# A fourth of the down products' weight remainders made by an adding transfer

## The chip, the cores and the metric

The kernel runs on one core of a Trainium2 chip. The metric is the device time of one execution in microseconds.

## The reference, cut to what matters

One decoder layer on 256 tokens of width 2048, in float32: a SwiGLU feed-forward network (FFN), a mixer with gated linear attention and dilated attention, and a second FFN.

```python
def swiglu(x, w_gate, w_up, w_down):
    return (jax.nn.silu(x @ w_gate) * (x @ w_up)) @ w_down
...
x = x + 0.5 * swiglu(rms_norm(x, ffn1_norm), ffn1_w_gate, ffn1_w_up, ffn1_w_down)
h = rms_norm(x, mix_norm)
z = h @ w_in
...
x = x + concat(o_g, o_a) @ w_out
x = x + 0.5 * swiglu(rms_norm(x, ffn2_norm), ffn2_w_gate, ffn2_w_up, ffn2_w_down)
```

The down products are `(...) @ w_down`, with w_down of 5632 x 2048, once in each FFN.

## The kernel before, in words

All large products are made in float32 precision out of three products in a rounded format (fp32r). Each operand W is split into a rounded part Wh and a remainder Wl = W - Wh, and the same is done with the activations; TensorE then adds activation-high x Wh (L179), activation-high x Wl (L181) and activation-low x Wh (L183) into one bank of PSUM. The helper `split` (L87 to L90) makes the two parts: the scalar engine copies W into a rounded tile (L89), and the vector engine subtracts that from W (L90).

The weights come as 1 MB pairs of tiles. `prepare` (L127) starts the load of a pair `raw` on SyncE's queue when it reaches the first tile of the pair (k = 0, L149; three buffers of raw), and then splits one of its two tiles, 128 x 1024, into `wh` and `wl`, four buffers of each. `weights` (L159) keeps two more tiles ready ahead of the one that it hands out. A list `jobs` (L114) gives the order of all weights: first FFN gate and up, first FFN down, the mixer, second FFN gate and up, second FFN down.

`column_pair` (L191) goes over the inner dimension, one weight tile at a time. With a tile it makes twelve matmuls: two halves of the tokens (t), three products, two banks (j). For a gate/up pair the inner dimension is 16 tiles, and eleven such pairs follow each other. For the down products it is 44 tiles, and two passes make the 2048 columns, so 88 weight tiles in each FFN.

At the end of a gate/up pair, for each t, `evac` (L231) makes sg (scalar engine, L233), u and its block transpose us (vector engine, L234, L238), and GpSimd issues 16 small transfers `ur<-us` of 16 KB that finish the transpose (L241). `finish`, run later, splits ur into the activations uh and ul of the down products. The last of these 32 transfers of a pair therefore fall into the beginning of the next pair, and those of the eleventh pair into the beginning of the down products. The transfers of GpSimd's queue use eight completion semaphores in turn, and an issue waits until the transfer eight places before it has landed.

The instructions of each engine are put in order when the program is built, by a scheduler that goes by dependencies and its own costs; after that each engine takes its own in order.

Of the kernel before, what the change touches and what calls it, by code (L numbers as in the profile page):

```python
# [14 lines left out]
F32 = mybir.dt.float32  # L15
F32R = mybir.dt.float32r
U32 = mybir.dt.uint32
AF = mybir.ActivationFunctionType
ALU = mybir.AluOpType
# [17 lines left out]
def layer_kernel(tc, x, xT, gains, gla_gate_up, gla_gate_bias, gla_out_norm, att_q_norm, att_k_norm,  # L37
                 w_ff1, w_dn1, w_mix, w_low, w_out, w_ff2, w_dn2, c_sq, c_rope, c_mask, out):

    nc = tc.nc  # L40
# [3 lines left out]
    with ExitStack() as es:  # L44
# [42 lines left out]
        def split(dst_h, dst_l, src):  # L87

            nc.scalar.activation(dst_h, src, AF.Copy)  # L89
            nc.vector.tensor_sub(dst_l, src, dst_h.bitcast(F32))  # L90
# [30 lines left out]
        raws = [None]  # L121
        started = []

        def wtile(name):
            return wp.tile([P, 2, 512], F32R, name=name, tag=name, bufs=WBUF)

        def prepare():  # L127
            if not jobs:
                return
            job = jobs.pop(0)  # L130
            if job == "low":
                raw = wp.tile([P, KT, P], F32, name="raw", tag="raw", bufs=3)
                nc.sync.dma_start(raw, w_low.rearrange("p (k f) -> p k f", f=P))
                got = []
                for i in range(2):
                    w = wtile("wh").rearrange("p j f -> p (j f)").rearrange("p (k f) -> p k f", f=P)
                    nc.gpsimd.memset(w.bitcast(F32), 0.0)
                    split(w[:, :, 0:RANK], w[:, :, 64:64 + RANK], raw[:, 8 * i:8 * i + 8, 0:RANK])
                    got.append(w)
                ready.extend(got)  # L140
                return
            w, i, k = job
            if k == 0:
                raw = raws[0] = wp.tile([P, 2, 2, 512], F32, name="raw", tag="raw", bufs=3)
                flat = raw.rearrange("p k j f -> p (k j f)")
                parts = 1 if started else 4
                started.append(True)
                for c in range(0, 2048, 2048 // parts):
                    nc.sync.dma_start(flat[:, c:c + 2048 // parts], w[i, :, c:c + 2048 // parts])  # L149
            wh, wl = wtile("wh"), wtile("wl")  # L150
            if len(started) < 3:
                started.append(True)
                for j in range(2):
                    split(wh[:, j], wl[:, j], raws[0][:, k, j])
            else:
                split(wh, wl, raws[0][:, k])
            ready.append((wh, wl))

        def weights(early=False):  # L159
            if early:  # L160
                return prepare()
            while jobs and len(ready) <= AHEAD:
                prepare()
            return ready.pop(0)
# [511 lines left out]
```

## Time and profile before

| | before |
|---|---|
| median of 3 runs | 1766.66 us (1765.84 to 1767.97) |
| the profiled execution | 1767.72 us |
| its span in the profile | 1765.9 us |
| TensorE busy | 1757.9 us |
| VectorE busy | 994.3 us |
| ScalarE busy | 838.5 us |
| GpSimd busy | 375.3 us |
| granted TensorE clock, mean | 0.999 |

PE is TensorE, DVE the vector engine, ACT the scalar engine, POOL GpSimd, and SPq SyncE's queue of transfers. A row of a group ends with its busy time, the mean length of one instruction in ns, and the idle time of its engine just ahead of it with what ended that. The busy time of GpSimd counts the issue of a transfer, not its movement; the time from issue to landing stands in a list of its own.

### The profile page before, as it was taken

Reading aid. Unit: us, or ns where it says so; the run is one execution under the profiler, and the core shown is the slowest. Engines: PE = TensorE matmul, PEld = TensorE weight load, DVE = VectorE, ACT = ScalarE, POOL = GpSimd, SP = SyncE. Lnnn points to the kernel's source line nnn. Section 1 sums busy time; section 2 is a strip of 40 time slices with the busy share of each in tenths; the row PEclk is TensorE's granted clock in tenths of the full one; section 3 lists DMA queues with packets and bytes.
Section 4 is the critical chain, followed back from the end, with each engine's and each line's share of the span. In section 5 each row is a group of like instructions: output and inputs, shape, how many; then the busy total and the mean of one; then the engine's idle time right before and its main releaser. Section 6 shows DMA issues by size and latency. Waiting matters only on the chain.

```text
span 1765.9 us, 21578 instructions
## 1 busy us (share of the span) xinstructions
PE 1757.9 (100%) x8276; PEld 1535.6 (87%) x8276; DVE 994.3 (56%) x1045; ACT 838.5 (47%) x1014; POOL 375.3 (21%) x742
## 2 busy tenths in 40 slices
PE   9999999999999999999999999999999999999999
PEld 7888888888888888888888888888888888888887
DVE  6555555555544645566655666555555555544544
ACT  6444444444444544565754454444444444444442
POOL 0333343443400001011000000333333343410000
PEclk9999999999999999999999999999999999999999
DMA  8666666666655556555444455666666566565653
GB/s 335 211 218 213 216 214 219 207 225 220 213 213 197 193 210 209 193 198 212 167 167 163 148 193 197 218 214 216 215 214 218 212 220 213 212 215 211 219 211 119
DMA packets 74695, 365.45 MB, mean 207 GB/s; under 512 B 17200, under 2 KB 30512, under 8 KB 32352
## 3 DMA queue, kind: packets, MB, share of 16 engines
q1 hardware_dynamic: 50864, 350.25, 55.5%
q0 software_dynamic: 23008, 12.76, 2.5%
q8 instruction: 64, 1.05, 0.2%
q10 hardware_dynamic: 720, 1.07, 0.2%
q14 instruction: 39, 0.32, 0.0%
HBM read 350.38 MB, written 2.10 MB: 200 GB/s over the span
## 4 chain that ended last, share of the span: by engine, by line
PE 99%; DMA 1%; DVE 0%; ACT 0%; SPq 0%; issue 0%
PE acc L181 32%; PE acc L183 32%; PE acc L179 32%; PE tp L85 1%; DMA raw<-in_w_ff_dram 0%; PE tp L540 0%; PE tp L402 0%; PE tp L555 0%; DMA gT<-in_gains_dram 0%; PE tp L558 0%; PE acc L455 0%; PE acc L456 0%; PE tp L428 0%; PE tp L427 0%; PE tp L477 0%; PE tp L520 0%
## 5 line engine op out<-in xcount | busy, mean ns | idle before, releaser
L90 DVE TENSOR_TENSOR wl<-raw,wh 128x1024 fp32r<-128x1024 f32 (+1 forms) x658 | 800.6, 1221 | 708.9 <-ACT wh L89 708.4
L89 ACT ACTIVATE wh<-raw 128x1024 fp32r<-128x1024 f32 (+1 forms) x660 | 690.8, 1051 | 862.9 <-PE acc L183 846.3
L181 PE MATMUL acc<-wl,hh 128*128 128x512 f32 x1792 | 549.2, 381 | 0.1
L183 PE MATMUL acc<-wh,hl 128*128 128x512 f32 x1792 | 544.6, 381 | 0.0
L179 PE MATMUL acc<-wh,hh 128*128 128x512 f32 x1792 | 536.1, 381 | 2.3 <-ACT wh L89 2.3
L241 POOL DMA_DIRECT2D ur<-us x704 | 344.3, 497 | 574.4 <-ACT sg L233 404.7
L179 PEld LDWEIGHTS acc<-wh,hh 128*128 128x128 f32 x1792 | 338.3, 189 | 51.0 <-ACT wh L89 3.1
L181 PEld LDWEIGHTS acc<-wl,hh 128*128 128x128 f32 x1792 | 338.7, 189 | 49.0 <-issue 1.0
L183 PEld LDWEIGHTS acc<-wh,hl 128*128 128x128 f32 x1792 | 338.9, 189 | 47.8 <-DVE hl L276 0.2
L181 PE MATMUL acc<-wl,uh 128*128 128x512 f32 x704 | 212.4, 379 | 0.0
L183 PE MATMUL acc<-wh,ul 128*128 128x512 f32 x704 | 211.9, 379 | 0.0
L179 PE MATMUL acc<-wh,uh 128*128 128x512 f32 x704 | 210.7, 379 | 0.0
L183 PEld LDWEIGHTS acc<-wh,ul 128*128 128x128 f32 x704 | 133.1, 189 | 18.9
L181 PEld LDWEIGHTS acc<-wl,uh 128*128 128x128 f32 x704 | 133.1, 189 | 18.8
L179 PEld LDWEIGHTS acc<-wh,uh 128*128 128x128 f32 x704 | 133.0, 189 | 18.6
L106 POOL TENSOR_TENSOR rs<-a,mhalf 128x4 f32<-128x4 f32 (+1 forms) x12 | 17.5, 1455 | 257.0 <-DVE a L352 257.0
L320 POOL DMA_DIRECT2D rope<-in_c_rope_dram x1 | 0.7, 747 | 209.1 <-PE acc L183 209.1
L234 DVE SCALAR_TENSOR_TENSOR u<-acc,rt,sg 128x512 f32<-128x512 f32 x44 | 32.7, 744 | 0.0
L238 DVE STREAM_TRANSPOSE us<-u 128x512 f32<-128x512 f32 x44 | 31.3, 711 | 1.5
L106 POOL TENSOR_TENSOR rt<-ssum,mhalf 128x1 f32<-128x1 f32 x6 | 3.9, 644 | 123.9 <-DVE ssum L110 123.8
L233 ACT ACTIVATE sg<-acc,rt 128x512 f32<-128x512 f32 x44 | 29.8, 678 | 0.6
L90 DVE TENSOR_TENSOR ul<-ur,uh 128x512 fp32r<-128x512 f32 x44 | 30.1, 683 | 0.0
(151 smaller groups left out, 598.0 us busy)
## 6 DMA issues: line engine op xcount, KB each, us to landing
raw<-in_w_ff_dram SPq DMA_DIRECT2D x175, 1024.0 KB, 5.0
raw<-in_w_dn_dram SPq DMA_DIRECT2D x88, 1024.0 KB, 4.8
raw<-in_w_mix_dram SPq DMA_DIRECT2D x48, 1024.0 KB, 4.8
raw<-in_w_out_dram SPq DMA_DIRECT2D x16, 1024.0 KB, 4.8
ur<-us POOLq DMA_DIRECT2D x704, 16.0 KB, 3.9
xs<-in_x_dram SPq DMA_DIRECT2D x2, 1024.0 KB, 9.5
xt<-in_xT_dram SPq DMA_DIRECT2D x7, 256.0 KB, 6.8
raw<-in_w_ff_dram SPq DMA_DIRECT2D x4, 256.0 KB, 4.3
```

Source lines behind the costliest of these rows:

```text
L85: nc.tensor.transpose(dst, src, ident[:n, :n])
L89: nc.scalar.activation(dst_h, src, AF.Copy)
L90: nc.vector.tensor_sub(dst_l, src, dst_h.bitcast(F32))
L106: nc.gpsimd.tensor_tensor(dst, src, mhalf[:, :src.shape[-1]], op=ALU.pow)
L179: nc.tensor.matmul(ps[j], lhsT=sh, rhs=alt(wh[:, j, :]), start=first and i == 0, stop=False)
L181: nc.tensor.matmul(ps[j], lhsT=sh, rhs=alt(wl[:, j, :]), start=False, stop=False)
L183: nc.tensor.matmul(ps[j], lhsT=sl, rhs=alt(wh[:, j, :]), start=False, stop=last and i == len(ws) - 1)
L233: nc.scalar.activation(halves(sg), ps[0], AF.Silu, scale=rt[:, t:t + 1])
L234: nc.vector.scalar_tensor_tensor(halves(u), ps[1], rt[:, t:t + 1], halves(sg), op0=ALU.mult, op1=ALU.mult)
L238: nc.vector.transpose(us.rearrange("p (q j c) -> p j q c", q=4, j=4), u)
L241: nc.gpsimd.dma_start(ur[32 * q:32 * q + 32, r * P:(r + 1) * P], us[32 * r:32 * r + 32, q * P:(q + 1) * P])
L320: ld(rv, c_rope.rearrange("(t p) f -> p t f", p=P))
```

## The change

In the down products of both FFNs, for every second pair of tiles (i odd) the second tile (k = 1) is split in another way. The scalar engine copies W rounded into wh as before, copies -W rounded into wl, and GpSimd issues a transfer from raw onto wl that adds: wl becomes -Wh + W. The vector engine has no part in it. That is every fourth tile (tiles 3, 7, 11 and so on), 22 of the 88 in each FFN. The lines behind the new branch move down by five: L179, L181, L183, L233 and L241 of before are L184, L186, L188, L238 and L246 of after.

```diff
                 for j in range(2):
                     split(wh[:, j], wl[:, j], raws[0][:, k, j])
+            elif k and i % 2 and (w is w_dn1 or w is w_dn2):
+
+                nc.scalar.activation(wh, raws[0][:, k], AF.Copy)
+                nc.scalar.activation(wl, raws[0][:, k], AF.Copy, scale=-1.0)
+                nc.gpsimd.dma_start(wl.bitcast(F32), raws[0][:, k], accum_op=ALU.add)
             else:
                 split(wh, wl, raws[0][:, k])
             ready.append((wh, wl))
```

GpSimd's instructions from the first FFN to the mixer, before: the 352 small transfers of eleven pairs, then loads for the mixer.

```order
L106 ISA
L106 TENSOR_TENSOR rt<-ssum,mhalf 128x1 x2
L241 DMA ur<-us 32x128 x352
L320 DMA rope<-in_c_rope_dram 128x2x128
L321 DMA gq<-in_att_q_norm_dram 128x128
```

And now (wl<-raw is the adding transfer):

```order
L106 TENSOR_TENSOR rt<-ssum,mhalf 128x1 x2
L246 DMA ur<-us 32x128 x320
L159 DMA wl<-raw 128x1024
L246 DMA ur<-us 32x128 x32
L159 DMA wl<-raw 128x1024 x21
L325 DMA rope<-in_c_rope_dram 128x2x128
```

The first adding transfer (tile 3) stands ahead of the 32 small transfers of the eleventh pair, and the second (tile 7) with all the others behind them. The second FFN has the same rows.

The scalar engine around the end of the eleventh pair of the first FFN, before (sg is that pair's evacuation, uh its activations):

```order
L233 ACTIVATE sg<-acc,rt 128x512
L89 ACTIVATE wh<-raw 128x1024
L233 ACTIVATE sg<-acc,rt 128x512
L89 ACTIVATE wh<-raw 128x1024 x7
L89 ACTIVATE uh<-ur 128x4x128
L89 ACTIVATE wh<-raw 128x1024 x6
L89 ACTIVATE uh<-ur 128x4x128
```

And now (L158 is the negated copy):

```order
L238 ACTIVATE sg<-acc,rt 128x512
L158 ACTIVATE wl<-raw 128x1024
L157 ACTIVATE wh<-raw 128x1024
L238 ACTIVATE sg<-acc,rt 128x512
L89 ACTIVATE wh<-raw 128x1024 x3
L158 ACTIVATE wl<-raw 128x1024
L157 ACTIVATE wh<-raw 128x1024
L89 ACTIVATE wh<-raw 128x1024 x3
L89 ACTIVATE uh<-ur 128x4x128 x2
```

The negated copy stands ahead of the plain one of the same tile, and both splits of the last activations have moved to one place.

TensorE at tile 7 of the first FFN's down products, before (acc_3772 and acc_3773 are the banks of the first half of the tokens, acc_3780 and acc_3781 those of the second; wh_3856 and wl_3857 are tile 7):

```order
L179 MATMUL acc_3772<-wh_3856,uh_122 128x512
L179 MATMUL acc_3773<-wh_3856,uh_122 128x512
L181 MATMUL acc_3772<-wl_3857,uh_122 128x512
L181 MATMUL acc_3773<-wl_3857,uh_122 128x512
L183 MATMUL acc_3772<-wh_3856,ul_123 128x512
```

And now (tile 7 is wh_3857 and wl_3858):

```order
L184 MATMUL acc_3772<-wh_3857,uh_122 128x512
L184 MATMUL acc_3773<-wh_3857,uh_122 128x512
L184 MATMUL acc_3780<-wh_3857,uh_122 128x512
L184 MATMUL acc_3781<-wh_3857,uh_122 128x512
L186 MATMUL acc_3772<-wl_3858,uh_122 128x512
```

The remainder's first product has moved from the third to the fifth matmul of this tile. In the second FFN the same holds for tile 7 and for two later tiles of the adding kind, and at the very last tile the order of the last four was written anew; in the other tiles of the adding kind the remainder stands where it stood.

## The prediction

> **What bounds the kernel now.** I read the page first: busy times, the chain that ended last and the groups of the two engines that split the weights.
>
> ```profile
> span 1765.9 us, 21578 instructions
> ...
> PE 1757.9 (100%) x8276; PEld 1535.6 (87%) x8276; DVE 994.3 (56%) x1045; ACT 838.5 (47%) x1014; POOL 375.3 (21%) x742
> ...
> PE 99%; DMA 1%; DVE 0%; ACT 0%; SPq 0%; issue 0%
> ...
> L90 DVE TENSOR_TENSOR wl<-raw,wh 128x1024 fp32r<-128x1024 f32 (+1 forms) x658 | 800.6, 1221 | 708.9 <-ACT wh L89 708.4
> L89 ACT ACTIVATE wh<-raw 128x1024 fp32r<-128x1024 f32 (+1 forms) x660 | 690.8, 1051 | 862.9 <-PE acc L183 846.3
> ```
>
> The list of transfers (KB each, us from issue to landing at the end):
>
> ```profile
> raw<-in_w_dn_dram SPq DMA_DIRECT2D x88, 1024.0 KB, 4.8
> ...
> ur<-us POOLq DMA_DIRECT2D x704, 16.0 KB, 3.9
> xs<-in_x_dram SPq DMA_DIRECT2D x2, 1024.0 KB, 9.5
> ...
> rope<-in_c_rope_dram POOLq DMA_DIRECT2D x1, 128.0 KB, 2.5
> ```
>
> TensorE is busy for 1757.9 of 1765.9 us, so at most 8.0 us could be won by removing all its idle time. The vector engine sits idle waiting for the scalar engine, and the scalar engine waits for TensorE to give a weight buffer back (846.3 us). Both are ahead of TensorE, not behind it. Freeing the vector engine gives the kernel nothing; the question is only whether the new source of a remainder is as early as the old one.
>
> How early it must be is read from the timeline of TensorE at the start of the down products of the first FFN (columns: start, length, engine, line, operation, tiles, count).
>
> ```profile
> 465.73 0.59 PE L181 MATMUL acc<-wl,hh 128*128 128x512 f32 x2
> 466.16 0.59 PE L183 MATMUL acc<-wh,hl 128*128 128x512 f32 x2
> 466.59 0.59 PE L179 MATMUL acc<-wh,uh 128*128 128x512 f32 x2
> ...
> 474.79 0.59 PE L181 MATMUL acc<-wl,uh 128*128 128x512 f32 x2
> ...
> 484.72 0.59 PE L179 MATMUL acc<-wh,uh 128*128 128x512 f32 x2
> 485.15 0.59 PE L181 MATMUL acc<-wl,uh 128*128 128x512 f32 x2
> 485.58 0.59 PE L183 MATMUL acc<-wh,ul 128*128 128x512 f32 x2
> ```
>
> The down products start at 466.59. A weight tile is twelve matmuls; from tile 0 at 466.59 to tile 7 at 484.72 are 18.13 us, 2.59 us a tile. Four buffers are in turn: tile 3's remainder goes where the last gate/up tile's was, which is read until 465.73 + 0.59 = 466.32, and it is first read at 474.79. That is a budget of 8.47 us, the same for every fourth tile after.
>
> **The change, part by part.**
>
> *Removed:* 44 subtractions (22 in each FFN) of 1.22 us, 54 us of the vector engine, all beside TensorE: worth 0. *Added on the scalar engine:* 44 copies of -W, rounded, 1.05 us each, 46 us in two phases of 88 x 2.59 = 228 us on an engine that is busy for 47% of the span: 0 by themselves, but each lies in the budget above. *Added on the GpSimd queue:* 44 transfers of 512 KB, which must read W and -Wh and write the sum. No row shows one, so its time L from issue to landing is an unknown. The ends are the 128 KB rope load at 2.5 us and the 1 MB load of x in the crowded start, 9.5. The nearest row is a weight load, 4.8 us: it moves 1 MB once, and the new transfer reads twice 512 KB. I add 0.7 for GpSimd's longer issue (rows below) and for other loads in flight, and take **L = 5.5**.
>
> Beside that row stands a rule of the Trainium skill ("DMA: Bandwidth & Descriptors", Anatomy of one DMA): a transfer from GpSimd costs about 2.0 us fixed plus bytes at 436 GB/s. By it 512 KB would take an estimated 3.2 us and, with both sources counted, 4.4. It gives 4.4 for a weight load too, and the row has 4.8, so the row is taken; with 3.2 for L the forecast below would be some 4.6 us lower.
>
> *Does L fit in steady running?* The scalar engine, the vector engine and GpSimd at the same place show what a handover takes.
>
> ```profile
> 464.20 1.06 ACT L89 ACTIVATE wh<-raw 128x1024 fp32r<-128x1024 f32 x1 [1.53 <-PE acc L183]
> ...
> 465.29 1.23 DVE L90 TENSOR_TENSOR wl<-raw,wh 128x1024 fp32r<-128x1024 f32 x1 [1.36 <-ACT wh L89]
> ...
> 467.21 0.71 DVE L238 STREAM_TRANSPOSE us<-u 128x512 f32<-128x512 f32 x1
> ...
> 468.46 4.88 POOL L241 DMA_DIRECT2D ur<-us  x10 [20.35 <-ACT sg L233]
> 474.69 4.89 POOL L241 DMA_DIRECT2D ur<-us  x10 [1.34 <-DMA ur<-us]
> 481.24 5.98 POOL L241 DMA_DIRECT2D ur<-us  x12 [1.66 <-DMA ur<-us]
> ```
>
> And GpSimd's groups of issues (busy time, mean ns of one):
>
> ```profile
> L241 POOL DMA_DIRECT2D ur<-us x704 | 344.3, 497 | 574.4 <-ACT sg L233 404.7 <-DMA ur<-us 80.2 <-issue 76.7
> ...
> L320 POOL DMA_DIRECT2D rope<-in_c_rope_dram x1 | 0.7, 747 | 209.1 <-PE acc L183 209.1
> ```
>
> In the timeline the transpose ends at 467.92 and the first issue begins at 468.46: 0.54 us. So 8.47 - 1.05 (the copy) - 0.54 - 0.15 (two handovers; from the scalar to the vector engine, 465.26 to 465.29, it took 0.03, and I estimate twice that or more from a transfer's landing) leaves **6.7 us for L**. At 5.5 it fits: 0. It also holds raw longer than the subtraction did. Raw has three buffers, so the copy of the next tile in that buffer is five tiles (12.95 us) behind; the release after 1.05 + 0.54 + 5.5 = 7.1 and a load of 4.8 make 11.9, so 0 is taken there too.
>
> *The queue it is put on.* GpSimd issues in order. Behind the last gate/up column pair stand the 32 small transfers of its two halves (the timeline's rows above: 10 + 10 + 12), and in the changed program the first accumulating transfer (tile 3) is ahead of all 32, the second (tile 7) behind all 32. Before, only the splits of the last activations waited for them, which the down products read at the end of a pass (tiles 40 to 43). They end at 481.24 + 5.98 = 487.22. Tile 7's remainder is wanted earlier: in the new order it is that tile's fifth matmul, at 485.58. So it is late before it is even issued, by 487.22 - 485.58 = 1.64 us.
>
> How the first transfer moves the 32: its negated copy can start at 466.32, ends about 467.4, and is issued about 467.95, for about 0.6 us, so the small ones start near 468.5, as now. They use eight completion semaphores in turn, so the eighth behind it waits for it to land, at 467.95 + 5.5 = 473.45, where now it starts near 468.46 + 7 x 0.497 = 471.94: 1.5 later. Part of that falls into the waits of 1.34 and 1.66 us that are there already. The ends are 3.0 earlier (both waits gone) and 4 later (a landing of 8 us); I take **1.0 later**.
>
> Tile 7 then: 1.64 + 1.0 + 5.5 + 0.1 (to TensorE) = **8.2 us** in which TensorE stands. Queued behind that waiting matmul is everything TensorE has; nothing else can fill in, since it takes its matmuls in order.
>
> The same place in the second FFN:
>
> ```profile
> 1533.72 0.59 PE L179 MATMUL acc<-wh,uh 128*128 128x512 f32 x2
> ...
> 1552.71 0.59 PE L183 MATMUL acc<-wh,ul 128*128 128x512 f32 x2
> ...
> 1552.07 2.44 POOL L241 DMA_DIRECT2D ur<-us  x5 [0.21 <-issue]
> ```
>
> The small transfers end at 1554.51, the fifth matmul of tile 7 is at 1552.71: 1.80 + 6.6 = **8.4 us**.
>
> *What a stop of TensorE costs beyond itself.* The only stop of the run in full work is at its start, 1.99 us for a weight. The stages behind it (columns: PE, PEld, DVE, ACT, POOL busy, granted clock, DMA share, GB/s) are:
>
> ```profile
> 13.84 1.13 PE L179 MATMUL acc<-wh,hh 128*128 128x512 f32 x4 [1.99 <-ACT wh L89]
> ...
> 14.00:16.00 2.00, 1.87 (x6) 1.32 (x7) 2.00 (x2) 1.61 (x4) 0.00 (x0) 0.74 1.05 416
> 16.00:18.00 2.00, 2.00 (x6) 1.55 (x6) 1.96 (x4) 2.00 (x3) 0.00 (x0) 0.50 0.96 394
> 18.00:20.00 2.00, 2.00 (x10) 1.72 (x9) 2.00 (x4) 1.64 (x3) 0.00 (x0) 0.91 1.09 419
> ```
>
> The clock was 0.74, 0.50 and 0.91 for 2 us each: 2 x (0.26 + 0.50 + 0.09) = **1.7 us** lost. A stop of 8 us is longer, so it is charged after each; the ends are 0 and twice that.
>
> After the stop tile 7's buffer goes its usual round and the third transfer (tile 11) finds GpSimd's queue empty. In the changed order of the last four tiles the remainder is put 41 matmuls behind its predecessor, as everywhere, so 0 there.
>
> **Sum:** (8.2 + 1.7) + (8.4 + 1.7) = 20.0 us. The profiled execution took 1767.72 us for a span of 1765.9; it was 1.06 above the median of the three runs, 1766.66. 1766.66 + 20.0 = **1786.7 us**, +1.1%.
>
> **The rivals.** *Every transfer is late.* If L is over 6.7 us, TensorE waits at 42 of the 44 (all but the two tile 7s), L - 6.7 each time, and the two start stops grow by what L has over 5.5. With L = 8.1: 42 x 1.4 = 59, plus 20.0 + 2 x 2.6 = 25, so 84 us, 1851 us. At 9.5 it would be 146 us, 1912 us. For it speaks that a 16 KB transfer now takes 3.9 us in the median beside the weight loads, longer than 128 KB of rope took alone, so sharing costs; against it, that the transfer itself holds back the load of its raw buffer, so that less is in flight beside it. For a slow addition the Trainium skill ("Collectives: The Full Stack", Why ReduceScatter is half of AllGather) says that an add costs two source reads rather than arithmetic, and so halves the rate; that is an estimated 2.4 us of movement for 512 KB. No row here shows it. Chance 0.28.
>
> *Not slower: the queue clears in time.* One mechanism would do it. The small transfers run without their waits, from 468.5 with 32 x 0.497 = 15.9 to 484.4, and the accumulating one lands as fast as the fastest small one (1.6 us), at 486.0. It decides at a landing by about 486: the stop is then 0.5 us, too short for the clock to matter, and both FFNs cost 1 us, 1768 us.
>
> ```profile
> DMA to landing us min/median/max: 1.6/3.8/5.3
> ...
> POOL ur L241 <- DMA ur<-us: 3.0, 2, 1.7
> ```
>
> Against it: the waits and the landing depend on the same DMA engines, and 1.6 is for a thirty-second of the bytes. Even with all the waits gone, L must stay under 2 us, below the rope's 2.5. That the issue order on the chip is not what the program lists, so that the second transfer goes ahead of the small ones, would give the same time. Chance 0.10.
>
> *Faster* would need a shorter start or end, since the 8.0 us of idle lie there, and the change touches neither: 0.02.
>
> **How the numbers follow.** Forecast 0.60: two stops, 1778 (L = 2.5, no shift: 2 x (4.3 + 1.7) = 12) to 1800 (L = 6.7, a shift of 4: 20 + 2 x 4.2 = 28, and the clock charged up to twice). The range goes up to the first rival at L = 8.1, 1850, which holds some 0.2 of its 0.28, and leaves out the rest of it and the times near no change. This kernel's runs spread by 0.1%, so 0.2% (3.5 us) is what can be told from no change. Faster 0.02, same 0.10, slower 0.88.
>
> **What would show it.** Right: in each FFN one idle time of TensorE of 6 to 12 us at L186 in tile 7, released by a DMA into wl, with GpSimd's 32 small transfers and then the second accumulating one just ahead; a lowered clock for some 4 us behind it; no other idle time of TensorE in the down products; landing times of wl<-raw of 4 to 6.7 us. The first rival shows in landings over 6.7 and idle time at L186 all through the down products. Wrong altogether: TensorE as busy as before through both starts, or the time lost outside the down products.

## The result, and the profile after

The changed kernel takes 1809.35 us (median of 4 runs, 1804.72 to 1811.79) against 1766.55 before: the ratio is 1.0239, 95% interval 1.0226 to 1.0251, so 42.8 us slower. The forecast was 1786.7, 20 us slower. The profiled execution took 1807.12 us for a span of 1805.3, 39.4 us more than the span before. Nearly all of it lies in the down products: from their first matmul to their last they take 243.3 us in the first FFN and 253.2 us in the second, where 229.8 and 228.1 were taken before.

The page after: busy times, the group of TensorE that waits, the two new groups, and the transfers.

```profile
PE 1768.5 (98%) x8276; PEld 1537.3 (85%) x8276; DVE 940.9 (52%) x1001; ACT 880.1 (49%) x1058; POOL 413.2 (23%) x786
...
L186 PE MATMUL acc<-wl,uh 128*128 128x512 f32 x704 | 216.9, 386 | 27.4 <-DMA wl<-raw 27.2
...
L159 POOL DMA_DIRECT2D wl<-raw x44 | 37.5, 853 | 439.9 <-ACT wl L158 427.4
L158 ACT ACTIVATE wl<-raw 128x1024 fp32r<-128x1024 f32 x44 | 46.5, 1056 | 67.1 <-PE acc L186 67.0
...
raw<-in_w_dn_dram SPq DMA_DIRECT2D x88, 1024.0 KB, 5.1
...
wl<-raw POOLq DMA_DIRECT2D x44, 512.0 KB, 5.9
```

The vector engine is 53 us less busy and the scalar engine 42 us more, near the 54 and 46 of the forecast; neither shows on TensorE. The remainder's product now waits 27.2 us for the adding transfer. Before, the last number of its row was 0.0:

```profile
L181 PE MATMUL acc<-wl,uh 128*128 128x512 f32 x704 | 212.4, 379 | 0.0
```

What TensorE waited for after the change (us in total, times, longest; the two waits of the second row lie in the first 14 us of the run):

```profile
PE acc L186 <- DMA wl<-raw: 27.2, 15, 10.0
PE acc L184 <- ACT wh L89: 1.7, 2, 1.3
```

The first row is fifteen stops, of which two are large. GpSimd and TensorE around the first of them, in the first FFN:

```profile
466.06 0.92 POOL L159 DMA_DIRECT2D wl<-raw  x1 [20.00 <-ACT wl L158]
466.66 3.80 POOL L246 DMA_DIRECT2D ur<-us  x7
471.06 3.93 POOL L246 DMA_DIRECT2D ur<-us  x8 [0.60 <-DMA wl<-raw]
477.00 8.31 POOL L246 DMA_DIRECT2D ur<-us  x17 [2.00 <-DMA ur<-us]
485.30 0.94 POOL L159 DMA_DIRECT2D wl<-raw  x1
```

```profile
483.06 1.03 PE L184 MATMUL acc<-wh,uh 128*128 128x512 f32 x4
490.71 1.22 PE L186 MATMUL acc<-wl,uh 128*128 128x512 f32 x2 [6.62 <-DMA wl<-raw]
491.72 1.06 PE L188 MATMUL acc<-wh,ul 128*128 128x512 f32 x2
492.57 1.06 PE L186 MATMUL acc<-wl,uh 128*128 128x512 f32 x2
493.43 1.06 PE L188 MATMUL acc<-wh,ul 128*128 128x512 f32 x2
494.28 1.04 PE L184 MATMUL acc<-wh,uh 128*128 128x512 f32 x2
495.13 0.61 PE L186 MATMUL acc<-wl,uh 128*128 128x512 f32 x2
```

The second adding transfer is issued at 485.30, straight behind the last of the 32 small ones. It lands at 490.7, and TensorE has stood for 6.62 us. The pairs of matmuls behind the stop take 0.86 us each instead of 0.43, until 495. In the second FFN the same stop is 10.04 us. Ahead of the last five of the 32 small transfers GpSimd stands idle there for 2.50 us, ended by nothing that the profile names; the last section comes back to that.

```profile
1568.97 2.44 POOL L246 DMA_DIRECT2D ur<-us  x5 [2.50 <-issue]
1571.41 0.94 POOL L159 DMA_DIRECT2D wl<-raw  x1
...
1575.93 1.22 PE L186 MATMUL acc<-wl,uh 128*128 128x512 f32 x2 [10.04 <-DMA wl<-raw]
```

The granted clock behind both (columns: PE, PEld, DVE, ACT, POOL busy, granted clock, DMA share, GB/s):

```profile
490.00:492.00 2.00, 1.29 (x3) 1.11 (x4) 0.33 (x1) 0.00 (x0) 0.00 (x0) 0.50 0.19 33
492.00:494.00 2.00, 2.00 (x6) 1.55 (x6) 0.00 (x0) 0.33 (x1) 0.00 (x0) 0.50 0.85 336
494.00:496.00 2.00, 2.00 (x8) 1.64 (x7) 0.00 (x0) 1.68 (x2) 0.86 (x1) 0.71 0.37 156
...
1576.00:1578.00 2.00, 2.00 (x5) 1.64 (x6) 0.00 (x0) 0.00 (x0) 0.00 (x0) 0.50 0.46 82
1578.00:1580.00 2.00, 2.00 (x6) 1.55 (x6) 0.00 (x0) 1.11 (x2) 0.00 (x0) 0.50 1.03 434
1580.00:1582.00 2.00, 2.00 (x10) 1.72 (x9) 0.00 (x0) 0.89 (x1) 0.85 (x1) 0.85 0.20 43
```

Work lost to the clock: 1.29 x 0.5 + 2 x 0.5 + 2 x 0.29 = 2.2 us, and 1.0 + 1.0 + 0.3 = 2.3 us. So the two starts cost 6.6 + 10.0 + 2.2 + 2.3 = 21.2 of the 39.4 us. The other 18.2 us lie later: thirteen stops of 0.2 to 2.5 us, 10.5 us together; 1.7 us of lower clock behind the longest of them (0.60 and 0.54 from 1686 to 1690); and short waits around them. In the first FFN they begin in the last third of the second pass, in the second FFN already at tile 39, near the end of the first pass. There the landing time, which I had as one number, is not one:

```profile
DMA to landing us min/median/max: 4.4/5.9/10.1
```

Read one by one, the landings of the first FFN go with how much of a weight load is still in flight at the issue. A released raw buffer lets one weight load start as soon as the adding transfer lands; the next load is issued 0.4 to 2.8 us behind it, and it is the one still moving when the following adding transfer is issued:

| adding transfer issued | second weight load of the pair: issued, landed | still in flight beside it | adding transfer's landing |
|---|---|---|---|
| 506.20 | 502.4, 508.4 | 2.2 us | 4.6 us |
| 516.56 | 512.8, 518.9 | 2.4 | 4.9 |
| 526.92 | 523.2, 529.4 | 2.5 | 5.8 |
| 537.28 | 533.5, 540.0 | 2.7 | 5.2 |
| 547.64 | 543.9, 550.9 | 3.2 | 5.7 |
| 558.00 | 554.2, 562.0 | 4.0 | 6.4 |
| 568.36 | 565.0, 572.7 | 4.3 | 6.8 |
| 578.72 | 575.7, 583.4 | 4.7 | 7.2 |
| 589.64 | 586.5, 593.4 | 3.8 | 6.2 |
| 601.05 (second pass) | 598.4, 603.4 | 2.4 | 4.8 |

A later landing starts the first load of the next pair later, the second moves beside it and lands later, and the next adding transfer meets more of it: on the whole it grows from turn to turn. The boundary between the passes, where two adding transfers stand up to 11.4 us apart instead of 10.4, sets it back. In the first FFN's first pass it comes just short of TensorE's need (7.2 us); in the second FFN it is over it at tile 39 (7.5). The first FFN's second pass is another case: five landings of 4.5 to 5.0 us follow each other without growth, until one transfer is issued 3 us late (656.23; see the last section). The two loads behind it then start 0.4 us apart, and the next transfer lands in 8.6 us.

### The profile page after: what moved, and what is told of

It reads as the page before. It is cut to its first block, busy times and chain, and to the rows that moved or that the text cites. A ratio compares the mean times of both kernels' runs of the same rounds, so it can differ in the third digit from the quotient of the medians.

```text
span 1805.3 us, 21765 instructions
## 1 busy us (share of the span) xinstructions
PE 1768.5 (98%) x8276; PEld 1537.3 (85%) x8276; DVE 940.9 (52%) x1001; ACT 880.1 (49%) x1058; POOL 413.2 (23%) x786
## 5 line engine op out<-in xcount | busy, mean ns | idle before, releaser
L90 DVE TENSOR_TENSOR wl<-raw,wh 128x1024 fp32r<-128x1024 f32 (+1 forms) x614 | 746.8, 1221 | 779.7 <-ACT wh L89 779.2
L89 ACT ACTIVATE wh<-raw 128x1024 fp32r<-128x1024 f32 (+1 forms) x616 | 644.2, 1050 | 778.3 <-PE acc L188 756.9
L186 PE MATMUL acc<-wl,hh 128*128 128x512 f32 x1792 | 548.2, 381 | 0.1
L188 PE MATMUL acc<-wh,hl 128*128 128x512 f32 x1792 | 543.7, 380 | 0.0
L184 PE MATMUL acc<-wh,hh 128*128 128x512 f32 x1792 | 536.2, 381 | 1.7 <-ACT wh L89 1.7
L246 POOL DMA_DIRECT2D ur<-us x704 | 345.2, 504 | 533.8 <-ACT sg L238 381.5
L184 PEld LDWEIGHTS acc<-wh,hh 128*128 128x128 f32 x1792 | 338.3, 189 | 50.4 <-ACT wh L89 2.7
L186 PEld LDWEIGHTS acc<-wl,hh 128*128 128x128 f32 x1792 | 338.3, 189 | 48.7 <-issue 1.0
L188 PEld LDWEIGHTS acc<-wh,hl 128*128 128x128 f32 x1792 | 338.3, 189 | 47.8
L186 PE MATMUL acc<-wl,uh 128*128 128x512 f32 x704 | 216.9, 386 | 27.4 <-DMA wl<-raw 27.2
L188 PE MATMUL acc<-wh,ul 128*128 128x512 f32 x704 | 214.5, 383 | 0.0
L184 PE MATMUL acc<-wh,uh 128*128 128x512 f32 x704 | 211.0, 381 | 0.0
L186 PEld LDWEIGHTS acc<-wl,uh 128*128 128x128 f32 x704 | 133.3, 192 | 53.5 <-DMA wl<-raw 35.0
L188 PEld LDWEIGHTS acc<-wh,ul 128*128 128x128 f32 x704 | 134.7, 191 | 19.5
L184 PEld LDWEIGHTS acc<-wh,uh 128*128 128x128 f32 x704 | 134.0, 190 | 19.2
L159 POOL DMA_DIRECT2D wl<-raw x44 | 37.5, 853 | 439.9 <-ACT wl L158 427.4
L158 ACT ACTIVATE wl<-raw 128x1024 fp32r<-128x1024 f32 x44 | 46.5, 1056 | 67.1 <-PE acc L186 67.0
L157 ACT ACTIVATE wh<-raw 128x1024 fp32r<-128x1024 f32 x44 | 45.8, 1040 | 0.0
## 6 DMA issues: line engine op xcount, KB each, us to landing
xs<-in_x_dram SPq DMA_DIRECT2D x2, 1024.0 KB, 10.1
```

The source lines that it names most:

```text
L157: nc.scalar.activation(wh, raws[0][:, k], AF.Copy)
L158: nc.scalar.activation(wl, raws[0][:, k], AF.Copy, scale=-1.0)
L159: nc.gpsimd.dma_start(wl.bitcast(F32), raws[0][:, k], accum_op=ALU.add)
L184: nc.tensor.matmul(ps[j], lhsT=sh, rhs=alt(wh[:, j, :]), start=first and i == 0, stop=False)
L186: nc.tensor.matmul(ps[j], lhsT=sh, rhs=alt(wl[:, j, :]), start=False, stop=False)
L188: nc.tensor.matmul(ps[j], lhsT=sl, rhs=alt(wh[:, j, :]), start=False, stop=last and i == len(ws) - 1)
```

## The experiments

**Where the loss sits.** Two runs divide it: one without the second adding transfer of each FFN, one with only the first two.

```diff
-            elif k and i % 2 and (w is w_dn1 or w is w_dn2):
+            elif k and i % 2 and i != 3 and (w is w_dn1 or w is w_dn2):
```

> Tile 7 of each FFN (the second adding transfer) goes back to the vector engine; the other 42 stay. Theory (two start stops plus late stops that grow out of bunched weight loads): the stops of 6.6 and 10.0 us at tile 7 and the slow clock behind them (2.3 and 2.6) are gone, the late stops stay: 1809 - 21 = 1788 us. Rival (every adding transfer costs TensorE about 1 us, wherever it stands): 1809 - 2 = 1807 us.

Measured: 1793.49 us, ratio 1.0141 (1.0121 to 1.0161). Both large stops are gone, and the late ones are more (21 stops, the longest 2.1 us; landings up to 9.3):

```profile
PE acc L186 <- DMA wl<-raw: 18.9, 21, 2.1
```

```diff
-            elif k and i % 2 and (w is w_dn1 or w is w_dn2):
+            elif k and i % 2 and i <= 3 and (w is w_dn1 or w is w_dn2):
```

> Only tiles 3 and 7 of the first pass and of the second pass of each FFN that lie in the first two odd pairs are made by adding transfers, 4 transfers in all instead of 44. Theory: the two start stops stay whole, nothing else is late: 1766.6 + 21 = 1788 us. Rival (a price for each transfer): 1766.6 + 4 = 1771 us.

Measured: 1785.68 us, ratio 1.0109 (1.0094 to 1.0124), with two stops:

```profile
490.80 1.22 PE L186 MATMUL acc<-wl,uh 128*128 128x512 f32 x2 [6.96 <-DMA wl<-raw]
```

Four transfers cost 19 us; 42 transfers, without tile 7, cost 27 us. By the two intervals each of these can be off by some 3 us, so the sum, 46, cannot be told from the whole 42.8. In the profiled executions the late stops are longer without tile 7 (18.9 us against 10.5), most of it in the first FFN, where they begin at 529 us instead of 672; that the long stop lets the loads come apart would explain it, but in the second FFN, after one stop of 0.8 us at tile 11, they begin no earlier (1674 against 1661), and no run tests it. A price for each transfer is refuted by both runs.

**Which transfers must wait behind which.** The 32 small transfers of the last pair go onto SyncE's queue.

```diff
-                                nc.gpsimd.dma_start(ur[32 * q:32 * q + 32, r * P:(r + 1) * P],
+                                (nc.sync if b == FF // 512 - 1 else nc.gpsimd).dma_start(ur[32 * q:32 * q + 32, r * P:(r + 1) * P],
```

> All 44 adding transfers stay, but the 32 small transfers of the last gate/up pair go onto SyncE's queue, so that the second adding transfer has nothing ahead of it on GpSimd's. Theory (the start stops are the wait behind the 32): the second adding transfer is issued about 478 instead of 485.3, the stops of 6.6 and 10.0 us at tile 7 are gone; the fifth weight load now stands behind the 32 and may cost up to 2 us at tile 8; the late stops stay at the 27 us of the run without tile 7: about 1794 us. Rival (tile 7 is late for another reason, say the first use of a buffer): the stops stay and the time is 1807 us or more.

Measured: 1820.62 us, ratio 1.0301 (1.0276 to 1.0326): slower still. The second adding transfer is issued at 478.22, counted from the start of its pass 9 us sooner than in the changed kernel, lands in 4.6 us, and tile 7 is in time. But the 32 take 22 us on SyncE's queue and the fifth weight load stands behind them, so the stop moves to tile 8's weights and is longer:

```profile
468.10 22.38 SPq L246 DMA_DIRECT2D ur<-us  x32
490.59 8.90 SPq L149 DMA_DIRECT2D raw<-in_w_dn_dram  x4
```

```profile
PE acc L186 <- DMA wl<-raw: 22.1, 22, 2.1
PE acc L184 <- ACT wh L89: 21.5, 4, 10.2
```

The theory held on tile 7; I priced the place behind the 32 at 2 us, and it is 10. On SyncE's queue the issues follow each other at some 0.6 us, nearly without waits; on GpSimd's, 32 x 0.50 us and the waits for landings made some 20 us. Either way a stretch of 32 issues holds up what stands behind it.

**What makes a landing long.** First the hold on raw: the transfer takes its second addend from Wh.

```diff
-                nc.gpsimd.dma_start(wl.bitcast(F32), raws[0][:, k], accum_op=ALU.add)
+                nc.gpsimd.dma_start(wl.bitcast(F32), wh.bitcast(F32), accum_op=ALU.add)
```

> The 44 transfers add Wh instead of W onto -Wh (the remainder becomes 0 in these tiles: that part of the computation is left out). Bytes, queue and addition are the same, but raw is given back by the scalar engine's copies. Theory (late stops come from the loads that wait for raw and then bunch): landing times stay at 4.4 to 5.5 us through the whole pass, no late stops, the two start stops stay: about 1788 us. Rival (the transfer slows because its bytes compete with the loads, wherever raw stands): landings up to 8 us and late stops as before: 1809 us.

Measured: 1914.87 us, ratio 1.084 (1.0815 to 1.0866). My theory, as I put it there, fell, and the rival was too mild:

```profile
PE acc L186 <- DMA wl<-wh: 110.7, 42, 19.9
```

```profile
DMA to landing us min/median/max: 4.4/8.8/10.4
```

With raw given back by the copies, the next weight load is issued at the very time of the adding transfer (load 497.5, transfer 497.81), each of them meets a whole load, and nearly every landing (39 of 44) is 8.3 to 10.4 us. The edit also did two things that were not meant. The transfer is issued one copy later, since Wh must be there first, and the program's new order puts the first adding transfer (tile 3) behind the 32 small ones (issued at 487.98), so that the two start stops alone are 16.5 and 19.9 of the 110.7 us. The other 74 us of stops come with the long landings. So the hold on raw is not what makes a landing long; it keeps that load away. What makes it long is a weight load beside it.

That was tested from the other side: the down products' loads bring half the bytes. The copies and the adding transfer read that half too, in lines left out here.

```diff
-                for c in range(0, 2048, 2048 // parts):
+                for c in range(0, 1024 if half else 2048, 1024 if half else 2048 // parts):
...
-                split(wh, wl, raws[0][:, k])
+                split(wh, wl, raws[0][:, 0 if half else k])
```

> The weight loads of the down products bring only the first half of each pair, and both tiles of a pair are made from it (half of the down weights are left out); the 44 adding transfers are unchanged. Theory (an adding transfer lands in 4.4 us alone, and in up to 8 to 10 beside a weight load): with loads half as long the landings stay at 4.4 to 5.5 us, no late stops; the start stops stay: about 1787 us. Rival (the transfer grows slow by itself, in its ring or its addition): landings of 7 to 9 us and 1805 us or more.

Measured: 1789.17 us, ratio 1.0121 (1.0104 to 1.0138). Landings are 4.4 in the median and 6.6 at most, and only the two start stops are left:

```profile
PE acc L187 <- DMA wl<-raw: 14.4, 2, 8.7
```

```profile
DMA to landing us min/median/max: 4.3/4.4/6.6
```

Next, the addition itself: a plain copy in its place.

```diff
-                nc.gpsimd.dma_start(wl.bitcast(F32), raws[0][:, k], accum_op=ALU.add)
+                nc.gpsimd.dma_start(wl.bitcast(F32), raws[0][:, k])
```

> The 44 transfers copy W onto wl instead of adding it (the remainder is replaced by W there: the subtraction is left out). One source is read instead of two. If the second read is what makes the landing 4.4 us at best, it falls to about 3.3 us, loads bunch less, late stops vanish and the start stops shrink by 1 us each: about 1785 us. If the landing is set by fixed costs and the queue, it stays at 4.4 us and more and the time at 1805 to 1809 us.

Measured: 1785.34 us, ratio 1.0104 (1.0089 to 1.0119).

```profile
PE acc L186 <- DMA wl<-raw: 11.9, 2, 6.0
```

```profile
DMA to landing us min/median/max: 2.8/2.9/6.3
```

The copy lands in 2.8 us, so reading and adding a second source is 1.6 us of the 4.4. With 2.8 the loads seldom bunch (behind a late issue at 656.54, with a landing of 6.3 us, they do, and come apart again within a few turns), and the late stops vanish; the start stops stay.

Then the other tile of the pair, which should have spread the loads.

```diff
-            elif k and i % 2 and (w is w_dn1 or w is w_dn2):
+            elif not k and i % 2 and i != 3 and (w is w_dn1 or w is w_dn2):
```

> The first tile of every odd pair is made by an adding transfer instead of the second (tile 6 of the first pass left to the vector engine), 42 transfers. Raw is then given back by the subtraction of the second tile, at nearly the time of the kernel before, so loads come evenly, one per 5.2 us. Theory (overlap with loads sets the landing): every transfer meets about one load, landings are an even 6 to 7.5 us without growth, stops of 0 to 0.5 us: 1767 to 1787 us. Rival (the hold on raw and the pairs of loads behind it are what makes it slow): landings of 4.4 to 5 us and no stops, 1767 to 1769 us.

Measured: 1809.9 us, ratio 1.0243 (1.0226 to 1.026), outside both expectations.

```profile
PE acc L186 <- DMA wl<-raw: 31.2, 27, 3.2
```

```profile
DMA to landing us min/median/max: 4.4/8.2/10.8
```

The loads did not come evenly: with landings of 8 us the transfer is again the last to release raw (two loads were issued at 506.1 and 506.5, right behind a landing at 506.1), and each transfer meets most of a load. The direction fits sharing, the size was not foreseen: moving the transfer by a tile moved it into the loads.

**Half as many.** Every eighth tile.

```diff
-            elif k and i % 2 and (w is w_dn1 or w is w_dn2):
+            elif k and i % 4 == 1 and (w is w_dn1 or w is w_dn2):
```

> Only every eighth tile (3, 11, 19 ...), 22 transfers. Theory: no transfer has the 32 small ones ahead of it when it is wanted, and the loads have 20.7 us to come apart again, so landings stay below 7 us: 1767 to 1770 us, as before the change. Rival (a price of about 0.6 to 1 us for each transfer): 1780 to 1789 us.

Measured: 1767.45 us, ratio 1.0004 (0.9995 to 1.0013): no difference from the kernel before. The second transfer (tile 11) is issued at 488.52, behind the 32 as well, but is not wanted before 495; landings are 4.3 to 6.6 us. The only wait that the profile lists is one of 0.5 us, of PEld, the loading of an operand into TensorE, and not of a matmul:

```profile
PEld acc L186 <- DMA wl<-raw: 0.5, 1, 0.5
```

**Is that all?** Two runs close the account: no transfer at all, with the copies kept, and both causes taken away at once.

```diff
-                nc.gpsimd.dma_start(wl.bitcast(F32), raws[0][:, k], accum_op=ALU.add)
```

> The 44 transfers are left out, and nothing takes their place (the remainder is -Wh there: the addition of W is left out); the 44 negated copies stay and the 44 subtractions stay gone. Theory (all of the loss comes from the transfers, none from the copies, and the vector engine's relief is worth nothing): 1766 to 1767 us. Rival (the extra copies hold up the scalar engine, or the relief wins something that the transfers hide): 1770 us and more, or 1764 us and less.

Measured: 1766.36 us, ratio 1.0001 (0.9991 to 1.001). The 44 further copies cost nothing, and the 53 us that the vector engine is spared win nothing.

The last run joins the edits of the half-length loads and of the run without tile 7.

```diff
+            half = w is w_dn1 or w is w_dn2
...
-            elif k and i % 2 and (w is w_dn1 or w is w_dn2):
+            elif k and i % 2 and i != 3 and (w is w_dn1 or w is w_dn2):
```

> Half-length weight loads in the down products (half of the down weights are left out) and tile 7 of each FFN left to the vector engine, 42 transfers. Theory (waiting behind the 32 small transfers and sharing the DMA engines with the weight loads are the only two causes): nothing is late, 1767 to 1769 us. Rival (a third cause): 1772 us or more.

Measured: 1768.41 us, ratio 1.0012 (1.0002 to 1.0021). With 42 of the 44 transfers in place, some 2 of the 42.8 us are left. The two causes account for the loss. Which resource a transfer and a load share, no run parts. No version beat the kernel before, and none had more than its 8.0 us of idle time to win.

## Why the prediction was half right

- *Freed vector engine worth 0, copies worth 0*: right, shown by the run without transfers (ratio 1.0001, 0.9991 to 1.001).
- *The queue it is put on*: right. The second adding transfer was issued straight behind the 32 small ones, and the stops were 6.62 and 10.04 us where 8.2 and 8.4 were forecast; the sum, 16.7 against 16.6, is closer than its parts. Counted from the start of the pass, the 32 were through 0.3 us earlier than before in the first FFN (1.0 later was taken) with a landing of 5.4 behind them, and 3.9 later in the second with a landing of 4.5. Of the 3.9, 2.5 are the idle time shown above; the run with four transfers has none there, and its second stop was 9.50 us all the same, by longer waits for landings among the 32 (6.3 us of idle time, where the first FFN of the changed kernel has 2.6). That the errors of the two FFNs nearly cancel is luck.
- *What a stop costs beyond itself*: right, 2.2 and 2.3 us where 1.7 was taken. The two starts together cost 21.2 against a forecast sum of 20.0.
- *"Does L fit in steady running? ... At 5.5 it fits: 0"*: this step failed. The budget was about right: landings up to 7.2 gave no stop, 7.3 one of 0.1 us, and 7.4 to 10.1 gave stops of 0.2 to 2.5, so the limit was 7.2 where 6.7 was worked out. The median landing, 5.9, was near 5.5 too. Wrong was to take L as one number. It is 4.4 us with half-length loads and 8.8 with a whole load beside every transfer, and in the changed kernel it runs through that span and crosses the budget late in each FFN. That term was 18.2 us of the profiled span, not 0, and it is nearly all of what the forecast of 20.0 lacked in that execution.
- *The first rival* ("every transfer is late", 0.28) was therefore partly true: 13 late stops, not 42. Against it I had written that the transfer holds back the load of its raw buffer, so that less is in flight beside it. The run that takes away the hold shows that this is so (1914.87 us without it). What I missed is the other half: the load that was held back then moves together with the next one, into the next transfer's time. I had the three release times in hand and checked only that a load would still be in time for its copy, not what it would meet on the way.
- *The Trainium skill's rules*: "DMA: Bandwidth & Descriptors" (Issuing engines are not separate DMA queues) says that transfers of all issuing engines share the same 16 DMA engines and interleave; the landings of 4.4 and 8.8 us for the same 512 KB agree, and it is the rule that I should have weighed in place of the fit for a lone transfer. The fit of that page of the Trainium skill gives an estimated 3.2 us for 512 KB, and the plain copy took 2.8; the estimate with both sources counted, 4.4, is what a quiet landing took. The Trainium skill gives that fit for GpSimd's path, and the weight load by which the prediction judged it goes on SyncE's queue. The Trainium skill's "Collectives: The Full Stack" (Why ReduceScatter is half of AllGather) puts the price of an add on its second read; the 1.6 us between copy and add fit that, but no run here parts reading from adding.
- *The range*: 1809 lies within 1778 to 1850 only because the range was drawn up to the first rival; the forecast's own story ended at 1800. That is luck too.

## What to carry to other kernels

A transfer that replaces work of an idle engine must be checked against three things: what stands ahead of it on its queue when it is first wanted, what other transfers are in flight at that moment, and which buffer it keeps from the next load. A landing time read from a quiet moment is a lower end; where two streams release each other's buffers, work out one full turn, with each stream's landing put into the other's start, and see whether it grows. Here every fourth tile grew out of its budget and every eighth stayed in it, at the same price for each transfer alone.

## What the runs showed of the hardware that was not expected

The accumulating transfer of 512 KB took 0.85 us to issue on GpSimd (37.5 us for 44), where a small one took 0.50. From the end of its copy to its issue passed 0.3 us in steady running, not the 0.54 that I had read before.

Once in the first FFN's second pass an issue came some 3 us late for no reason that the profile names (656.23 in the changed kernel, where the negated copy had ended at 653.00; it is at 656.54 with the plain copy and at 656.88 with half-length loads), and the next was on time. It goes by the place in GpSimd's queue, not by the tile. Counted from the queue's first transfer, this one is the 371st, and in the traces of all twelve kernels GpSimd pauses ahead of the 129th, 250th, 371st, 492nd and 613th transfer, and of the 734th where there is one: places 121 apart. The engine's idle time there is 2.4 to 2.9 us (1.7 in one trace) where nothing else is waited for. Where an adding transfer has the place, in eight cases, it is issued 3.23 us after the end of its copy instead of 0.3. In the changed kernel the 734th is among the 32 small transfers of the second FFN: that is the 2.50 us of idle time shown with the second stop. The kernel before has only 715 transfers on that queue. What the engine does in the pause, no trace shows.
